# Sliding windows by DMA alone: eleven and three quarters staged batches instead of eleven, a lower share of direct copies, and another order of the first load and the last stores

## The chip, the cores and the metric

The kernel runs on one core of one Trainium2 chip, the other cores idle. The metric is the device time of one execution in microseconds, as the median of several runs.

## The reference

The input is x of shape (32, 4096, 256) in float32. Each batch is cut into windows of 64 rows with a step of 32 rows, so neighbouring windows share half of their rows.

```python
n_windows = (length - window_size) // stride + 1        # 127
for i in range(n_windows):
    start = i * stride
    result[:, i] = x[:, start:start + window_size].copy()
```

In blocks of 32 rows (32 KB each), a batch is 128 blocks. Window w is block w followed by block w + 1, so every inner block is written twice. 134 MB come in and 267 MB go out. Nothing is computed.

## The kernel before

Two routes lead from x to the result.

- A *direct* copy goes from memory to memory. Each byte written costs one byte read, and it passes the DMA engines once (in the profiled run the two direct queues moved 174.83 MB, which is the 267.09 MB written less 92.27 MB of staged stores; with 46.14 MB of staged loads they make up the 220.95 MB read, to 0.02 MB). The synchronisation engine (SP) issues these, and the GpSimd engine (POOL) issues the last of them, called edges.
- A *staged* batch is loaded once into on-chip memory (SBUF), with one block per partition, and stored twice. It reads memory once for two writes, but the engines move three bytes where the direct route moves two (ACT's queue moved 138.41 MB for eleven batches, 12.58 MB each: 4.19 MB in and 8.39 MB out). The scalar engine (ACT) issues these: six loads, their twelve stores, then the second group of batches.

Eleven of 32 batches are staged. The code that the change touches, with cuts marked:

```python
    def load(self, q, g):                       # one staged batch: 128 partitions x 32 KB
        ...
        step = 128 // n
        parts = [(k, 4, 32, 1) for k in range(4)] if g == 0 else [(0, step, n, step)]
        for rows in parts:
            self.issue(self.c.load(q, self.tiles[i], b, c, rows), self.loaded[i])

    def store(self, q, g):                      # half 0 and half 1 of the windows
        ...
        parts, end = [((0, step, n, step), 0), ((0, step, n, step), 1)], []
        if g == len(self.items) - 1:
            parts = [((0, 1, 128, 1), 1), ((0, 1, 32, 1), 0)]
            end = [(96, 1, 32, 1)] + [(32 + k, 4, 16, 1) for k in range(4)]
...
    staged = [*range(1, B, 3)]
...
    first_loads, loads, stores = 6 * 17, 5 * 17, 6 * 34
    turns = share = 0
        st.run(ring_s)                          # the staged route, on ACT
        for i, (b, w) in enumerate(sixteens):   # the direct route, on SP, 16 windows at a time
            second = turns - first_loads - stores
            loading = turns < first_loads or 0 <= second < loads
            share += 120 if turns < 16 or -8 <= second < 16 else 90 if loading else 18
            if share >= 120:                    # two half copies: 2 packets + 2 completions
                share -= 120
                turns += 4
                count(c.windows(ring_d, b, w, 16, 0), done)
                count(c.windows(ring_d, b, w, 16, 1), sem)
            else:                               # a pair: 2 packets + 1 completion
                turns += 3
                count(c.windows(ring_d, b, w, 16), sem)
```

Both routes use the same 16 DMA engines (the three queues together fill 99% of their time, as the page below shows), and the mixture of pairs and half copies is the kernel's dial for how these are shared. The kernel counts on turns: every transfer of 16 or 32 KB and every completion write of 4 bytes as one, and two queues that both have work as getting equally many. The packet records show this: between 155 and 365 us SP's queue started 2458 packets and ACT's 2456 before (1559 and 2309 without the 4-byte ones). The 4-byte packets come to 16 for each copy (3264 for SP's 204 copies before). On average per engine, a pair moves 64 KB in 3 turns and two half copies move 64 KB in 4 turns. The staged queue moves sixteen packets of 16 KB in 17 turns, that is 15.06 KB a turn. So pairs alone give a direct share of 64 / (64 + 3 x 15.06) = 0.59 of the bytes, and half copies alone give 0.515.

## Time and profile before

| | before |
|---|---|
| time, median of 3 | 752.27 us (752.11 to 753.42) |
| bytes moved by the 16 engines | 313.26 MB |
| memory read / written | 220.95 / 267.09 MB |

From the page of the kernel before: the engines' busy tenths and rate in 40 slices, the queues (q1 is SP's, q10 ACT's, q0 POOL's; packets, MB, share of the 16 engines' time), memory traffic, and SP's issues of pairs (size, median us from issue to landing).

```profile
DMA  8999999999999999999999999999999999999996
GB/s 360 401 427 429 427 429 428 434 423 418 420 424 423 418 424 415 422 427 427 414 427 417 429 432 429 430 422 430 429 423 421 423 421 419 425 426 423 431 409 262
DMA packets 18290, 313.26 MB, mean 418 GB/s; under 512 B 4336, under 2 KB 4336, under 8 KB 4528
...
q1 hardware_dynamic: 8016, 154.32, 48.8%
q10 hardware_dynamic: 9104, 138.41, 44.0%
q0 software_dynamic: 1168, 20.51, 6.5%
...
HBM read 220.95 MB, written 267.09 MB: 651 GB/s over the span
...
out_dram<-in_x_dram SPq DMA_DIRECT2D x92, 1024.0 KB, 100.7
```

The three queues fill 48.8 + 44.0 + 6.5 = 99% of the engines' time, so there is no idle time to win outside the first and last slice. What can be won is in the GB/s row, which isn't flat.

From the windows view of the same run, the rate in five stretches (us, length, compute busy, clock, busy share of the 16 DMA engines, GB/s; a packet is counted where it starts, so that a share can come out at 1.01): start, loads beside direct copies, stores beside direct copies, second loads, second stores.

```profile
core 0: us, POOL busy (x), PEclk, DMA share, GB/s
5.00:37.00 32.00, 0.00 (x0) 1.00 1.01 408
30.00:110.00 80.00, 0.00 (x0) 1.00 1.01 428
155.00:365.00 210.00, 0.00 (x0) 1.00 1.01 421
450.00:495.00 45.00, 0.00 (x0) 1.00 1.01 431
560.00:630.00 70.00, 0.00 (x0) 1.00 1.01 423
```

The engines are busy all the time in each of them, yet stores run at 421 to 423 GB/s and loads at 428 to 431. The records of single packets say the same: the typical (median) 16 KB staged packet takes 611 ns and the typical 32 KB direct packet 1213 ns, but in the first store stretch SP's direct packets take about 1245 ns on average. Sixteen engines at 611 and 1213 ns move 429 and 432 GB/s; 431 is taken below as what the engines can move. Rates given "by the packet records" divide each packet over the time that it took, and so differ from the windows view by a few GB/s in short stretches.

The last lines before the end, same view:

```profile
709.00:733.00 24.00, 0.00 (x0) 1.00 1.01 414
736.00:740.00 4.00, 0.00 (x0) 1.00 0.97 413
740.00:744.00 4.00, 0.00 (x0) 1.00 0.63 259
```

### The profile page before, as it was taken

Reading aid. Unit: us, or ns where it says so; the run is one execution under the profiler, and the core shown is the slowest. Engines: PE = TensorE matmul, PEld = TensorE weight load, DVE = VectorE, ACT = ScalarE, POOL = GpSimd, SP = SyncE. Lnnn points to the kernel's source line nnn. Section 1 sums busy time; section 2 is a strip of 40 time slices with the busy share of each in tenths; the row PEclk is TensorE's granted clock in tenths of the full one; section 3 lists DMA queues with packets and bytes.
Section 4 is the critical chain, followed back from the end, with each engine's and each line's share of the span. In section 5 each row is a group of like instructions: output and inputs, shape, how many; then the busy total and the mean of one; then the engine's idle time right before and its main releaser. Section 6 shows DMA issues by size and latency. Waiting matters only on the chain.

```text
span 749.4 us, 322 instructions
## 1 busy us (share of the span) xinstructions
POOL 12.8 (2%) x26
## 2 busy tenths in 40 slices
POOL 0000000000000000000000000000000000040100
DMA  8999999999999999999999999999999999999996
GB/s 360 401 427 429 427 429 428 434 423 418 420 424 423 418 424 415 422 427 427 414 427 417 429 432 429 430 422 430 429 423 421 423 421 419 425 426 423 431 409 262
DMA packets 18290, 313.26 MB, mean 418 GB/s; under 512 B 4336, under 2 KB 4336, under 8 KB 4528
## 3 DMA queue, kind: packets, MB, share of 16 engines
q1 hardware_dynamic: 8016, 154.32, 48.8%
q10 hardware_dynamic: 9104, 138.41, 44.0%
q0 software_dynamic: 1168, 20.51, 6.5%
q14 instruction: 2, 0.02, 0.0%
HBM read 220.95 MB, written 267.09 MB: 651 GB/s over the span
## 4 chain that ended last, share of the span: by engine, by line
another core or an unknown queue 92%; POOL 2%; issue 0%; POOLq 0%; SPq 0%
POOL out_dram L34 2%; POOL out_dram L44 0%; POOLq L236 0%; SPq L172 0%; POOLq L114 0%
## 5 line engine op out<-in xcount | busy, mean ns | idle before, releaser
L34 POOL DMA_DIRECT2D out_dram<-in_x_dram x21 | 12.0, 576 | 691.3 <-DMA out_dram<-in_x_dram 654.0
L44 POOL DMA_DIRECT2D out_dram<-in_x_dram x1 | 0.6, 581 | 0.0
L222 POOL MEMSET const-float32-0.0<- 128x1 f32 x1 | 0.1, 98 | 0.2 <-issue 0.2
L222 POOL MEMSET const-bfloat16-1.0<- 128x1 bf16 x1 | 0.1, 101 | 0.0
L222 POOL MEMSET const-float32-1.0<- 128x1 f32 x1 | 0.1, 98 | 0.0
L222 POOL MEMSET const-uint8-127<- 128x1 uint8 x1 | 0.1, 98 | 0.0
## 6 DMA issues: line engine op xcount, KB each, us to landing
out_dram<-in_x_dram SPq DMA_DIRECT2D x92, 1024.0 KB, 100.7
out_dram<-xb ACTq DMA_DIRECT2D x21, 4096.0 KB, 139.7
out_dram<-in_x_dram SPq DMA_DIRECT2D x110, 512.0 KB, 90.3
xb<-in_x_dram ACTq DMA_DIRECT2D x10, 4096.0 KB, 131.4
out_dram<-in_x_dram POOLq DMA_DIRECT2D x20, 960.0 KB, 38.5
xb<-in_x_dram ACTq DMA_DIRECT2D x4, 1024.0 KB, 15.7
out_dram<-xb ACTq DMA_DIRECT2D x2, 1024.0 KB, 113.4
out_dram<-xb ACTq DMA_DIRECT2D x4, 512.0 KB, 96.9
```

The costliest lines, as they stand in the source:

```text
L34: return q.dma_start(out=self.oap((b * self.nw + w0) * 2 + h, [[2 * blk, n], row]), in_=self.xap(b * self.nb + w0 + h, [[blk, n], row]), m ...
L44: return q.dma_start(out=self.oap((b * self.nw + w0) * 2, [[part, 16], [2 * self.blk, n], row]), in_=self.xap(b * self.nb + w0, [[part, 16 ...
L222: nc = _bacc.Bacc("TRN2", target_bir_lowering=False, num_devices=1)
```

## The change

The intent is to move memory traffic off the direct route. Three quarters of batch 0 are staged too, and the direct share is lowered so that both routes still end together. The first batch is loaded in one copy. The last stores read every fourth partition, and every third edge is cut into 16 KB packets, so that the last stretch gets a lower direct share too.

```diff
+    def pieces(self, g):
+        b, c, n = self.items[g]
+        if n == 128:
+            return [(c, (0, 1, 128, 1))]
+        return [(c, (0, 2, 64, 2)), (c + 64, (1, 4, 32, 4))]
 ...
-        parts = [(k, 4, 32, 1) for k in range(4)] if g == 0 else [(0, step, n, step)]
+        for c, rows in self.pieces(g):
 ...
-            parts = [((0, 1, 128, 1), 1), ((0, 1, 32, 1), 0)]
-            end = [(96, 1, 32, 1)] + [(32 + k, 4, 16, 1) for k in range(4)]
+            parts = [(c, (0, 1, 128, 1), 1), (c, (0, 4, 32, 1), 0)]
+            end = [(k, 4, 32, 1) for k in (1, 2, 3)]
 ...
+    items.insert(6, (0, 1, c.nb * 3 // 4))
 ...
-    first_loads, loads, stores = 6 * 17, 5 * 17, 6 * 34
+    first_loads, loads, stores = 6 * 17, 5 * 17 + 14, 6 * 34
 ...
-            share += 120 if turns < 16 or -8 <= second < 16 else 90 if loading else 18
+            share += 120 if turns < 16 or -8 <= second < 16 else 116 if loading else 60
 ...
-            count(c.windows(ring_r, b, w, n), rest)
+            count(c.windows(ring_r, b, w, n, None, 16384 if i % 3 == 2 else DIRECT), rest)
 ... (the direct copies that batch 0 no longer needs; edges 112 to 116 and columns 117 to 124 of batch 30)
```

More of the change, by code (lines that the diff above doesn't have):

```diff
@@ L84, in issue @@
         self.count[sem] += 16
+    def pieces(self, g):
[3 more added lines that the diff above has]
+        return [(c, (0, 2, 64, 2)), (c + 64, (1, 4, 32, 4))]
     def load(self, q, g):
         i = g % len(self.tiles)
-        b, c, n = self.items[g]
         if self.count[self.stored[i]]:
             q.wait_ge(self.stored[i], self.count[self.stored[i]])
-        step = 128 // n
-        parts = [(k, 4, 32, 1) for k in range(4)] if g == 0 else [(0, step, n, step)]
-        for rows in parts:
-            self.issue(self.c.load(q, self.tiles[i], b, c, rows), self.loaded[i])
+        for c, rows in self.pieces(g):
+            self.issue(self.c.load(q, self.tiles[i], self.items[g][0], c, rows), self.loaded[i])
         self.after_load[g] = self.count[self.loaded[i]]
@@ L100, in store @@
         q.wait_ge(self.loaded[i], self.after_load[g])
-        step = 128 // n
-        parts, end = [((0, step, n, step), 0), ((0, step, n, step), 1)], []
+        parts, end = [(*piece, half) for half in (0, 1) for piece in self.pieces(g)], []
         if g == len(self.items) - 1:
-            parts = [((0, 1, 128, 1), 1), ((0, 1, 32, 1), 0)]
-            end = [(96, 1, 32, 1)] + [(32 + k, 4, 16, 1) for k in range(4)]
-        for rows, half in parts:
-            self.issue(self.c.store(q, self.tiles[i], b, c, rows, half), self.stored[i])
+            parts = [(c, (0, 1, 128, 1), 1), (c, (0, 4, 32, 1), 0)]
+            end = [(k, 4, 32, 1) for k in (1, 2, 3)]
+        for first, rows, half in parts:
+            self.issue(self.c.store(q, self.tiles[i], b, first, rows, half), self.stored[i])
         for rows in end:
@@ L162 @@
     for b in direct:
-        w = 15 if b - 1 in staged else 0
+        w = c.nb * 3 // 4 + 1 if b == 0 else 15 if b - 1 in staged else 0
         sixteens += [(b, w + 16 * j) for j in range((c.nw - w) // 16)]
-    singles = [(B - 1, c.nw - 1, 1)]
-    edges = [(b, 0 if b - 1 in staged else 112, 15) for b in direct[:-1]]
+    singles = [(0, 0, 0), (0, c.nb * 3 // 4, 1), (B - 1, c.nw - 1, 1)]
+    edges = [(b, 0 if b - 1 in staged else 112, 15) for b in direct[1:-1]] + [(0, 113, 14)]
     last = B - 2
-    edges.append((last, 112, 4))
-    first_loads, loads, stores = 6 * 17, 5 * 17, 6 * 34
+    edges.append((last, 112, 5))
+    first_loads, loads, stores = 6 * 17, 5 * 17 + 14, 6 * 34
     turns = share = 0
@@ L192 @@
         ring_r.wait_ge(near, 16)
-        for b, w, n in edges:
+        for i, (b, w, n) in enumerate(edges):
             for k in (b - 1, b + 1):
@@ L196 @@
                     st.wait_stored(ring_r, place[k])
-            count(c.windows(ring_r, b, w, n), rest)
-        count(c.columns(ring_r, last, 116, 9), rest)
+            count(c.windows(ring_r, b, w, n, None, 16384 if i % 3 == 2 else DIRECT), rest)
+        count(c.columns(ring_r, last, 117, 8), rest)
         st.wait_stored(ring_d, place[B - 1])
```

## The prediction

> **What bounds it.** Nothing computes: the page shows DMA at 9 tenths in all but the first and last of 40 slices, and the DMA queue table (48.8 + 44.0 + 6.5%) fills the 16 engines for 99% of the 749.4 us span. 313.26 MB are moved. In the packet records a 16 KB staged packet takes 611 ns at best, and a 32 KB direct packet 1213 ns, so 16 engines move 429 to 432 GB/s at most[...]. At 431 GB/s the bytes alone need 727 us. The other 22 us: 6 us before the first packet, about 3 us at the end while engines finish one by one (busy falls from 744 us), and 13 us of packets slower than their best.
>
> Where packets are slow is the lever. In the windows, loads beside direct copies (420 to 500 us) run at 430 GB/s with a direct share of 0.53; stores beside direct copies (120 to 390, 510 to 650 us) at 423 GB/s with 0.57. A direct byte is read and written in HBM, a staged one only one of the two, so HBM traffic is rate x (1 + share): 657 and 664 GB/s. In 10 us windows of the store stretches the rate falls with the share (correlation -0.7 to -0.8, slope -150 to -240 GB/s per unit of share). So memory traffic costs about 1.7% there.
>
> **What the change does.**
> 1. Three quarters of batch 0 are staged as well: 3.15 MB of HBM reading go, but the same 3.15 MB are added to what the engines move (316.4 MB). At 427 GB/s: +7.4 us, all on the bounding engines.
> 2. Direct share. [...] Counting turns: two half copies per 16 windows take 4 turns for the bytes one pair moves in 3. Pairs fall from 92 to 46. The share goes from about 0.57 to 0.545 in stores, 0.53 to 0.515 in loads. With the slope, stores rise from 423 to between 427 and 429 GB/s over some 430 us: -4.5 to -6 us. Loads are already at 428 to 430: -0.3 us.
> 3. First load in one piece of 128 partitions, not four of every fourth: the first 35 us ran at 385 to 405 GB/s in places with staged packets of 680 to 830 ns; if the piece shape causes it, -1 us. The new item uses such shapes (every second, every fourth partition) for 9.4 MB: +0 to +2 us.
> 4. Last stores every fourth partition instead of 32 neighbours, smaller packets in every third edge: from 714 to 740 us staged packets averaged 650 to 700 ns. -1 to -2 us, end stagger perhaps included.
>
> Sum: 7.4 - 5.2 - 0.3 - 1 - 1.7 + 0.7 = about 0. Staged and direct remain balanced at the end (my count of turns left when the direct ring ends: 65 staged before, 85 after, against 76 and 90 for the edges).
>
> **Prediction: 751 us, range 746 to 757.** Chances: faster by over 2% 0.01, within 2% 0.98, slower 0.01.
>
> **What would show it.** 316.4 MB moved; HBM read 217.8 MB; mean rate of the span 418 to 423 GB/s; store stretches at 427 to 429 GB/s with share 0.545 and 32 KB direct packets near 1222 ns rather than 1244; load stretches unchanged; staged packets after 715 us nearer 611 ns.
>
> **What would make it wrong.** If slow packets in stores come from addresses meeting in memory, not the share, step 2 gains nothing: 756. If the partly strided item is slow in both directions: 755 or more. If the cap on HBM traffic is harder than the slope says, stores reach 430 and it is 747.

7.4 - 5.2 - 0.3 - 1 - 1.7 + 0.7 comes to -0.1 us, the "about 0" of the text.

## The result

| | before | after |
|---|---|---|
| time, median of 6 | 752.32 us (752.11 to 755.21) | 753.73 us (753.03 to 755.01) |
| ratio | | 1.0013 (0.9996 to 1.003) |
| span of the profiled run | 749.4 us | 751.2 us |
| MB moved | 313.26 | 316.41 |

A ratio here is always the mean time of one kernel's runs over that of the other's runs of the same rounds, so it isn't quite the ratio of the medians. 1.4 us in the medians is the whole difference, and the interval of the ratio includes 1.

The page of the changed kernel, the same lines as before:

```profile
DMA  9999999999999999999999999999999999999995
GB/s 377 421 431 429 420 425 431 427 429 429 427 429 425 427 425 434 421 434 433 430 405 424 427 433 430 429 435 425 429 430 430 424 428 429 426 434 427 428 427 223
DMA packets 19506, 316.41 MB, mean 421 GB/s; under 512 B 4962, under 2 KB 4962, under 8 KB 5170
...
q10 hardware_dynamic: 9696, 147.85, 46.5%
q1 hardware_dynamic: 8432, 148.09, 46.3%
q0 software_dynamic: 1376, 20.45, 6.5%
...
HBM read 217.81 MB, written 267.09 MB: 645 GB/s over the span
...
out_dram<-in_x_dram SPq DMA_DIRECT2D x46, 1024.0 KB, 91.9
```

3.15 MB more are moved and 3.14 MB fewer are read from memory. Of SP's issues, 46 are pairs, where there were 92. The mean rate rose from 418 to 421 GB/s. The same five stretches:

```profile
5.00:37.00 32.00, 0.00 (x0) 1.00 1.02 435
30.00:110.00 80.00, 0.00 (x0) 1.00 1.01 426
155.00:365.00 210.00, 0.00 (x0) 1.00 1.01 428
450.00:495.00 45.00, 0.00 (x0) 1.00 1.00 429
560.00:630.00 70.00, 0.00 (x0) 1.00 1.00 428
```

Stores now run at 428, in the first stretch as in the second. The start gained too, and the loads changed by 2 GB/s at most, in spite of their lower share. The end:

```profile
709.00:733.00 24.00, 0.00 (x0) 1.00 1.00 427
736.00:740.00 4.00, 0.00 (x0) 1.00 0.91 330
740.00:744.00 4.00, 0.00 (x0) 1.00 0.73 294
```

The 709 to 733 stretch rose from 414 to 427 GB/s, but at 736 to 740 the rate is 330 where before it was 413. (The profiled run of the changed kernel is 1.8 us longer, so equal times aren't equally far from the end.)

The packet records give a full account. At 431 GB/s (the level of the best stretches) a stretch of known bytes would take bytes / 431; what it took beyond that is its loss. Bytes plus losses add up to the span by construction, so the table shows where each microsecond went in these two executions. It is one profiled run of each kernel, and runs of one kernel differ by 2 to 3 us, so terms of some tenths are not to be trusted. The stretches are cut at the landings of loads and stores of each kernel.

| part of the span | before, us | after, us |
|---|---|---|
| bytes / 431 GB/s | 726.8 | 734.1 |
| loss: until the first packet | 2.4 | 2.0 |
| loss: first staged load | 1.9 | 0.95 |
| loss: rest of the first loads | 1.2 | 1.3 |
| loss: first stores | 5.2 | 1.4 |
| loss: turn from stores to loads | 0.6 | 1.3 |
| loss: second loads | 0.5 | 0.3 |
| loss: second stores | 2.5 | 0.9 |
| loss: edges beside stores (654 to 733, 651 to 731) | 1.8 | 0.3 |
| loss: end (from 733, from 731) | 6.6 | 8.7 |
| span | 749.4 | 751.25 |

So 7.3 us of additional engine work bought back 5.4 us in stores, 1.4 us at the start and 1.5 us in the edges, and 0.7 us at the turn and 2.1 us at the end were given back: 7.3 - 5.4 - 1.4 - 1.5 + 0.7 + 2.1 = 1.8, with loads unchanged.

The packet records split the loss at the end further. In both runs 3.6 us of it pass after the last packet. Before, engines standing idle ahead of the last packet cost another 2.6 us and slow packets 0.4; in the changed kernel 4.0 and 1.1. So about 1.4 of the 2.1 us come from engines that finish far apart, and 0.7 from slow packets.

### The profile page after: what moved, and what is told of

Read it like the earlier page. It is cut to its first block, busy times and chain, and to the rows that moved or that the text cites. A ratio compares the mean times of both kernels' runs of the same rounds, so it can differ in the third digit from the quotient of the medians.

```text
span 751.2 us, 359 instructions
## 1 busy us (share of the span) xinstructions
POOL 12.8 (2%) x26
## 2 busy tenths in 40 slices
DMA packets 19506, 316.41 MB, mean 421 GB/s; under 512 B 4962, under 2 KB 4962, under 8 KB 5170
## 4 chain that ended last, share of the span: by engine, by line
another core or an unknown queue 92%; POOL 2%; issue 0%; POOLq 0%; SPq 0%
POOL out_dram L34 2%; POOL out_dram L44 0%; POOLq L241 0%; SPq L177 0%; POOLq L118 0%
```

## The experiments

The theory: the rate in a stretch is the smaller of what the engines move (431 GB/s) and what memory allows, where a direct byte counts twice (read and written) and a staged byte once. So with the direct share s, memory traffic is rate x (1 + s), and before, in stores, 421.2 x 1.572 = 662 GB/s (rate and share by the packet records). The memory counter over the whole run agrees that direct bytes are read from memory and staged stores are not: the two direct queues (154.32 + 20.51 MB) and eleven loads of 4.19 MB make 220.97 MB, and 220.95 MB were read. The rivals: the added item or the shifted addresses made stores faster, not the share; only stores suffer; or the form of the copies counts. Each run was timed in 5 rounds; all results were correct.

Chips: the chip of the first comparison is called A below. The runs below came in three groups of four, one chip each, here B (before: median 751.99 us of 11 runs), C (744.20 of 9) and D (754.41 of 11).

### The share alone (chip B)

```diff
 kernel before
-            share += ... else 90 if loading else 18
+            share += ... else 116 if loading else 60
```

> The kernel before with the new share of direct copies (116 and 60 in place of 90 and 18) and nothing else. Theory (the rate in the store stretches is set by the direct share, through memory traffic): 137 to 400 us runs at 427 to 429 GB/s with share 0.545 to 0.55, as in the changed kernel (428.6), not 422.8 as before; but with only 11 staged batches about 15 MB of direct edges are left alone at the end, where every byte is read and written, at 330 to 370 GB/s, so the time is 753 to 758 us. Rival (the extra item or the addresses it shifts raised the rate): the stores stay at 423 GB/s with the lower share.

Measured: 754.42 us, ratio 1.0036 (1.0017 to 1.0055). Windows of its profile: first stores, second stores, and the direct copies left at the end.

```profile
155.00:365.00 210.00, 0.00 (x0) 1.00 1.01 428
560.00:630.00 70.00, 0.00 (x0) 1.00 1.01 426
694.00:730.00 36.00, 0.00 (x0) 1.00 1.02 357
```

Stores run at 428 and 426 GB/s with a share of 0.544 (from the packet records), as in the changed kernel, with no batch added. So the share sets the rate in stores. The end pays: at 694 to 730 us, with a share of 0.87, the rate is 353 GB/s by the packet records, and 353 x 1.87 = 659, the same traffic as in the store stretches.

### The added item with the old shares (chip B)

```diff
 changed kernel
-            share += ... else 116 if loading else 60
+            share += ... else 90 if loading else 18
```

> The changed kernel with the old shares (90 and 18). Theory: store stretches back at 422 to 424 GB/s with share 0.57 although three quarters of batch 0 are staged; 316.4 MB; staged stores are left alone at the end, at 429 GB/s, without loss; 755 to 758 us, 2 to 5 us above the changed kernel. Rival (extra item or shifted addresses raise the rate): stores at 427 to 429 GB/s with the old share, and 751 to 754 us.

Measured: 756.96 us, ratio 1.0064 (1.0051 to 1.0078). First and second stores:

```profile
155.00:365.00 210.00, 0.00 (x0) 1.00 1.01 422
560.00:630.00 70.00, 0.00 (x0) 1.00 1.00 422
```

Back at 422 GB/s, with shares of 0.565 and 0.574, although the item is there. The addresses and the item are out as the cause of the faster stores. Staging more without lowering the share costs the bytes and buys nothing.

### The shares turned round (chip B)

```diff
 kernel before
-            share += ... else 90 if loading else 18
+            share += ... else 18 if loading else 116
```

> The kernel before with the shares turned round: 18 in loads (share 0.57), 116 in stores (0.515). Theory (memory traffic as a sum of reads and writes is capped): loads fall to 421 to 424 GB/s, stores rise to 430. Rival (only the mixture of stores with direct copies is slow, as writes weigh more): loads stay at 427 GB/s or more at share 0.57, stores rise. Time 753 to 760 us either way, for 15 MB of direct copies left alone at the end; the verdict is read from the stretches.

Measured: 762.18 us, ratio 1.0137 (1.0113 to 1.0160). First loads, first stores, second loads:

```profile
30.00:110.00 80.00, 0.00 (x0) 1.00 1.00 415
155.00:365.00 210.00, 0.00 (x0) 1.00 1.01 431
450.00:495.00 45.00, 0.00 (x0) 1.00 1.00 417
```

Loads fall to 415 to 417 with a share of 0.573 to 0.580, and stores reach 431 with 0.515. The rival that only stores suffer is out; loads suffer even more (414.7 x 1.573 = 652) and fell below the expected 421 to 424. The time was above the expected 753 to 760, as more was left alone at the end (the profile is of the slowest of the six runs, 766.32 us): from 700 to 740 us the rate was 345 GB/s with a share of 0.94, that is 669 GB/s of traffic.

### The same share by other means (chip B)

```diff
 changed kernel
             if share >= 120:
                 share -= 120
-                turns += 4
-                count(c.windows(ring_d, b, w, 16, 0), done)
-                count(c.windows(ring_d, b, w, 16, 1), sem)
+                turns += 5
+                count(c.windows(ring_d, b, w, 16, None, 16384), sem)
 (and share += 60, 58 or 30 in place of 120, 116 or 60)
```

> The changed kernel with the same shares made another way: no half copies at all; every copy is a pair, and a quarter of them (half in loads) are cut in 16 KB packets, which take 5 turns instead of 3. Theory (the share itself counts): stores at 427 to 429 GB/s with share 0.545, time within 0.4% of the changed kernel. Rival (the half copies, with their gap in the output, are what runs faster): stores at 423 GB/s at that same share, 756 to 759 us.

Measured: 752.66 us, ratio 1.0002 (0.9984 to 1.0020). First stores:

```profile
155.00:365.00 210.00, 0.00 (x0) 1.00 1.01 428
```

Without a single half copy the stores run at the same rate with the same share (0.541 and 0.545). So the form of the copies isn't the cause. (The changed kernel itself wasn't run on this chip, so "within 0.4% of the changed kernel" can't be checked there.) In all four runs the rate in stores goes with the share.

### The first load alone (chip C)

```diff
 kernel before
-        parts = [(k, 4, 32, 1) for k in range(4)] if g == 0 else [(0, step, n, step)]
+        parts = [(0, step, n, step)]
```

> The kernel before with one thing of the change: the first load in one copy of 128 partitions, not four of every fourth. Theory (the four-piece load makes staged packets slow and starts the staged queue less early): 5 to 40 us at 427 to 429 GB/s as in the three kernels with the new load, not 409 to 416 as in the three with the old; the time falls by 1 to 2 us, 750 to 751.5 where before is 752. Rival (the head differs because of what else changed): 410 to 416 GB/s and no gain.

Measured: 745.56 us where before took 744.20, ratio 1.0017 (1.0004 to 1.0029). Start and first stores:

```profile
5.00:37.00 32.00, 0.00 (x0) 1.00 1.01 435
155.00:365.00 210.00, 0.00 (x0) 1.00 1.01 427
```

The start is fast, as expected, and yet the time didn't fall. Two things were wrong in the expectation. The staged queue now ran ahead, so its stores ended sooner and more direct copies were left at the end (373 GB/s from 729 to 735 us, the last 6 us in which all engines were busy, by the packet records). And this chip is another one: before takes 8 us less here, and with the old share of 0.572 stores run at 427, not 421 GB/s. 427.0 x 1.572 = 671 GB/s, where the other chips stop at 662.

### The old last stores (chip C)

```diff
 changed kernel
-            parts = [(c, (0, 1, 128, 1), 1), (c, (0, 4, 32, 1), 0)]
-            end = [(k, 4, 32, 1) for k in (1, 2, 3)]
+            parts = [(c, (0, 1, 128, 1), 1), (c, (0, 1, 32, 1), 0)]
+            end = [(96, 1, 32, 1)] + [(32 + k, 4, 16, 1) for k in range(4)]
```

> The changed kernel with the last stores as they were (32 neighbouring partitions, then 16 of every fourth). If the last stores on every fourth partition help: staged packets from 700 us slower than 611 ns (630 to 650 on average) and 1 to 2 us more, 754.5 to 756. If they cost time by leaving one engine late: the end 1 to 2 us earlier, 752. Rival (the last stores do not matter, the packets there were slow from the high share): staged packets at 611 to 620 ns, the time within 0.7 us of the changed kernel.

Measured: 748.45 us, ratio to before 1.0062 (1.0049 to 1.0076). The stretch of the last stores:

```profile
709.00:733.00 24.00, 0.00 (x0) 1.00 0.99 409
```

Staged packets between 709 and 733 us took 657 ns on average; in the next run, with the new last stores on the same chip, they took 613. Why stores from 32 neighbouring partitions should be slower isn't shown. The direct share was higher here too, 0.585 against 0.550, but at the 671 GB/s of traffic that the run before this one reached, that would cost about 2% (an estimate: 671 / 1.585 = 423 GB/s against 431), and the packets were 7% slower. Yet the time was not longer than the next run's, 748.67. That run differs in the dial as well, and the unedited changed kernel wasn't run on this chip, so what the last stores alone are worth in time isn't isolated; no gain from them is seen.

### A little more direct copying (chip C)

```diff
 changed kernel
-            share += ... else 116 if loading else 60
+            share += ... else 116 if loading else 54
```

> The changed kernel with 54 for 60: pairs a little more often in stores, so that some 1 MB more of stores is left when the direct ring ends. Theory (the last 16 us lose 5.1 us instead of 3.5 as the staged stores run out first on most engines and direct copies alone meet the memory limit): the stretch 738 to 746 us at 400 GB/s or more with share near 0.6, not 370 at 0.75; 1 to 1.5 us less in all, 752 to 753. Rival (the end is set by one late engine whatever the balance): no change in the time.

(The times in this text are 3.6 us late against the profile's clock, as the prediction's are; the reason is told further below.) Measured: 748.67 us, ratio to before 1.0063 (1.0050 to 1.0076). The last stores, and two stretches of the end:

```profile
709.00:733.00 24.00, 0.00 (x0) 1.00 1.00 427
736.00:740.00 4.00, 0.00 (x0) 1.00 0.52 213
740.00:744.00 4.00, 0.00 (x0) 1.00 0.06 25
```

The balance did improve: slow packets cost 0.2 us after 727 us, against 1.1 in the changed kernel (on chip A, after 731 us) and 0.6 in the run above (on this chip, after 726 us). But then the work of about one engine in sixteen (busy share 0.06) went on until 744; idle engines ahead of the last packet cost 5.0 us, and the loss of the end, counted as in the table, came out at 8.8 us where the changed kernel had 8.7. The time fits the rival, that the end is set by the last engine. It can't be compared with the changed kernel on this chip, and why an engine falls behind is open.

### Half a batch in place of three quarters (chip C)

```diff
 changed kernel
-    items.insert(6, (0, 1, c.nb * 3 // 4))
+    items.insert(6, (0, 1, c.nb // 2))
-            share += ... else 116 if loading else 60
+            share += ... else 90 if loading else 42
 (one piece of 64 partitions; windows and turns to match)
```

> A candidate: the changed kernel with half of batch 0 staged, not three quarters, and shares 90 and 42 (mean direct share 0.54 in place of 0.533). Estimate: 1.05 MB less moved gives 2.4 us, the higher share takes 1 to 2 us back, the balanced end gives 1 us: 750.5 to 752.5, so equal to before or up to 1.5 us faster. If the loss with the share is steeper than between the two kernels, 753 to 754.

Measured: 747.03 us, ratio 1.0039 (1.0026 to 1.0051). The first stores ran at 430.8 GB/s with a share of 0.551, by the packet records.

On this chip even a share of 0.56 costs nothing (431.5 GB/s in the second stores), so everything beyond eleven batches is only more bytes: 1.05 MB less than the last two runs is 2.4 us by the engines' rate, and 1.4 to 1.6 us was measured.

### The changed kernel once more (chip D)

No edit.

> The changed kernel itself, unedited, as its first comparison was on one chip only. The last four runs fell on a chip where before takes 744 us, not 752, and where stores run at 427 GB/s with share 0.57 and at 431 with 0.545 to 0.56. Theory (the change buys 3.15 MB of engine work, +7.3 us, with what memory traffic loses, and that loss is a property of the chip): where before takes 744 us the changed kernel is 0.5 to 0.7% slower (748 to 749); where before takes 752 us, within 0.3%. Rival (the ratio is that of the first comparison, 1.001, everywhere): 0.9996 to 1.003 on a 744 us chip too.

Measured: 755.33 us where before took 754.41, ratio 1.0004 (0.9978 to 1.0030). First stores, and a stretch of the end:

```profile
155.00:365.00 210.00, 0.00 (x0) 1.00 1.01 426
736.00:740.00 4.00, 0.00 (x0) 1.00 1.03 365
```

The 752 us case of the theory, repeated on a chip at least as slow; both the theory and the rival allow it, so this run doesn't decide between them. What the unedited kernel does on a chip such as C was not measured; the two nearest to it there, each with one part undone or one number moved, took 0.6% more than before.

### One level of the share, with and without the new first load (chip D)

```diff
 kernel before
-        parts = [(k, 4, 32, 1) for k in range(4)] if g == 0 else [(0, step, n, step)]
+        parts = [(0, step, n, step)]                     (first run only)
-            share += ... else 90 if loading else 18
+            share += ... else 40 if loading else 30      (44 and 36 in the second run)
```

> A candidate with no more bytes than before: 11 staged batches, first load in one piece, one level of the direct share (0.56) in loads and stores (40 and 30 in place of 90 and 18), the direct ring done a little sooner. Theory: on a 744 us chip 0.56 lies below the knee, so stores and loads both run at 430 GB/s or more and the time falls by 2 to 4 us to 740 to 742; on a 752 us chip stores gain about as much as loads lose (425 GB/s in both), 750 to 752. Rival (only stores suffer from the share; loads never): 1 to 2 us faster on either.

> The same level share (44 and 36) with the first load in four pieces as before; nothing else of before is changed. It tells what the first load is worth: if the one-piece load gains, this is 1 to 2 us slower than the run with it; if its gain is given back at the end (as in the run of the new load alone, 1.0017 of before), the two are equal within 0.7 us. On a 744 us chip 741 to 743 us, on a 752 us chip 750.5 to 752.5.

Measured: 755.89 us, ratio 1.0013 (0.9987 to 1.0039), with the new first load; 756.18 us, ratio 1.0022 (0.9990 to 1.0054), with the old. Neither beats before. Of the first run, the first loads and the first stores:

```profile
30.00:110.00 80.00, 0.00 (x0) 1.00 1.01 419
155.00:365.00 210.00, 0.00 (x0) 1.00 1.00 421
```

With a share of 0.56 the loads run at 419, the stores at 421, where lower shares gave first loads 425 to 429 on A, B and D; so loads lost, and stores gained little (421 with the old share on A). (The "knee" in the expectation is the share above which memory traffic binds.) On such a chip the level share is no better than the unequal shares of before; the intervals don't show that it is worse. The start with the new first load, and with the old:

```profile
5.00:37.00 32.00, 0.00 (x0) 1.00 1.01 429
5.00:37.00 32.00, 0.00 (x0) 1.00 1.01 418
```

That is on one chip and with nearly the same setting of the dial, but the share in this stretch came out at 0.526 and 0.557 by the packet records, so part of the gain at the start goes with the share and not with the shape of the copies. The times are equal within noise.

### Less staging than before (chip D)

```diff
 changed kernel
-    staged = [*range(1, B, 3)]
+    staged = [b for b in range(1, B, 3) if b != 16]
-            share += ... else 116 if loading else 60
+            share += ... else 40 if loading else 0
 (turns to match)
```

> The other direction: the changed kernel with batch 16 no longer staged, so 10.75 staged batches and 312.2 MB moved (4.2 MB less than the changed kernel, 1.05 less than before), with shares 40 and 0 (0.56 in loads, 0.587 in stores). Theory (time is the larger of bytes over 431 GB/s and memory traffic over the chip's cap, about 663 GB/s where before takes 752 us and 672 where it takes 744): stores at 417 to 419 GB/s on a 752 us chip and 755 to 757 us; at 422 to 424 and 744 to 746 us on a 744 us chip. Rival (fewer bytes always win, as the engines bound it): below before on both.

Measured: 759.70 us, ratio 1.0054 (1.0027 to 1.0082). Second stores:

```profile
560.00:630.00 70.00, 0.00 (x0) 1.00 1.00 413
```

The fewest bytes of all (312.2 MB) and slower. 417.5 x 1.577 = 658 and 414.0 x 1.588 = 657 GB/s of traffic: the engines don't bound it, and the traffic is what the theory gave. The rate in the second stores, 414, is below the expected 417 to 419, as their share was 0.588. The time is above the expected 755 to 757 by 2.7 us; the kernel before, too, took 2.4 us more than 752 on this chip.

### The law in one table

Share and rate in the first stores (155 to 365 us) from the packet records, and their product.

| run | chip | share | GB/s | rate x (1 + share) |
|---|---|---|---|---|
| shares turned round | B | 0.515 | 431.1 | 653 |
| share alone | B | 0.544 | 427.7 | 660 |
| old shares, item added | B | 0.565 | 421.8 | 660 |
| less staging | D | 0.577 | 417.5 | 658 |
| half a batch | C | 0.551 | 430.8 | 668 |
| first load alone | C | 0.572 | 427.0 | 671 |

On B and D the traffic in stores stops near 660 GB/s, on C near 672; the first and fifth rows, at 431 GB/s, are at the engines' limit instead. In loads on B and D with a share of 0.55 or more it is 649 to 661. One stretch doesn't fit: in the first loads of the changed kernel the share fell from 0.528 to 0.513 and the rate stayed where it was, 426.3 and 425.5 GB/s by the packet records, below both limits (427.3 with 0.513 on chip D). What holds it there is open.

Two simpler laws fail on the same records. A cap on reads or on writes alone: slow loads (shares turned round) read 415 and write 238 GB/s, slow stores (before) read 241 and write 421, direct copies alone (share alone, 709 to 733 us) do 335 of each; only the sums are near each other, 652, 662 and 667. And a fixed slower pace for each direct byte: between 431 GB/s with staged copies and 335 with direct copies alone, a share of 0.544 would give an estimated 373 GB/s, and 427.7 was measured.

## Why the prediction was right

The prediction was 751 us with 746 to 757; 753.73 was measured, and the verdict (within 2%) is right. The verdict alone says little about the mechanism: with no gain in stores at all the time would have been some 5.4 us, or 0.7%, longer, and still within 2%. The sum itself came to about 0, that is 752.3 us; the stated 751 is a microsecond lower without a reason. What tests the mechanism are the terms of the sum, one for each step:

- *Bytes, +7.4 us.* 7.3 us by the account. Right.
- *Stores, -4.5 to -6 us, from 423 to between 427 and 429 GB/s.* Measured 428 and -5.4 us; SP's 32 KB direct packets average 1225 ns in the first stores (predicted near 1222). That the share is the cause is shown by the first four runs, in the rate of the stores: changed alone it gives the gain, undone alone it takes the gain away, in loads a higher share does harm, and made by other means the lower share gives the same. That memory traffic stands behind the share is inferred, not counted by stretches: the product rate x (1 + share) stays between about 649 and 669 GB/s on chips B and D from a share of 0.56 up to 0.94, in loads, stores and direct copies alone.
- *Loads, -0.3 us.* About +0.1 and -0.2 us, within what one profile can tell.
- *First load, -1 us.* -1.4 us with the earlier first packet, in the account; but the start is not the time. Alone (chip C) the new load gained nothing in the time; more direct copies were left at the end.
- *The strided item, 0 to +2 us.* +0.7 us at the turn to the second loads, where its loads are. Part of that dip was there before (0.6 us), so its shape isn't shown to be the cause.
- *Last stores and edges, -1 to -2 us.* The step that was mis-sized: -1.7 us stood in the sum, and +0.6 was measured. The staged packets did fall to 611 ns between 709 and 733 us, and the edges beside stores gained 1.5 us (with a lower share as well, 0.540 in place of 0.586 at 694 to 730), but the end gave 2.1 us back. I wrote that the end stagger was "perhaps included". It grew instead: idle engines ahead of the last packet cost 4.0 us in place of 2.6, and slow packets cost 1.1 us in place of 0.4 where direct copies were left nearly alone (a share of 0.74 and 16 KB packets of 710 ns on average from 736 to 740 us; 0.58 and 614 ns before).
- *Balance at the end, counted in turns.* The count said that the staged queue would be 11 turns short of the edges before (65 against 76) and 5 after (85 against 90), so better balanced. In the packet records it is about 71 against 73 before and 77 against 86 after: it got worse. (Counted are packets and completions per engine that had still to start when SP's last 32 KB copies ended.) The staged turns of the changed kernel had been put about 8 too high, and at 736 to 740 us the direct share was 0.74.

One reading in the prediction was off: I had placed the packets so that the last one ends with the span. On the profile's clock they come 3.6 us earlier: the first packet starts 2.4 us after the span's start and the last ends 3.6 us before its end. So the "6 us before the first packet" are 2.4 us there and 3.6 us after the last one; the sum is the same, and "finish from 744 us" should read 740.

"What would make it wrong" named addresses as the rival; the run with the item and the old shares refutes it for the stores.

Where the expected gain of the change went, then: it was real, 5.4 us in stores, and the price was 7.3 us of engine work. The added staging turned memory traffic into engine work one for one (3.14 MB fewer read, 3.15 MB more moved). At the rates measured here, one MB of traffic less is worth an estimated 1 / 662 = 1.5 us where memory is the limit, and one MB more to move costs 1 / 431 = 2.3 us where the engines are. For 3.15 MB that is an estimate of 4.8 us, near the 5.4 us that stores gained, against 7.3 us; the start and the edges gave another 2.9 us, and the turn and the end took 2.8 us back. On chip C, at about 672 GB/s, stores lose less from the start (427 GB/s at the same share), so there is less to buy back; that this is why the variants there were 0.4 to 0.6% slower is argued, not tested. No version beat the kernel before on any chip tried. What stays open is why the last engine lags by some microseconds and why chips differ in memory traffic; only one chip of the second kind was seen.

## What to carry to other kernels

When two limits share the work (here engines and memory), look at each stretch for the one that binds, and work out the price of moving work from one to the other before moving it; near the balance point the trade can come out even: here 1.0% more bytes for the engines and 0.6% less memory traffic left the time the same. Here a share between two queues was set by counting turns (0.548 by the count, 0.539 to 0.547 measured), and its effect could be read as rate x (1 + share): 658 to 662 GB/s in the first stores of before (A), share alone and old shares (B) and less staging (D), 671 in those of the first load alone (C). Measure a change of less than one per cent on more than one chip: here the same old share cost 2% of the rate in stores on one chip and 1% on another.
